# Mixing layer of a hybrid encoder: V's products ahead of the scan's masked ones, masked products of four groups in one run, three scan outputs begun early

## The chip, the cores and the metric

The kernel runs on one core of a Trainium2 chip. The metric is the device time of one execution in microseconds (us); for each kernel the median of several runs is given, and one more execution is profiled. The engines are named as in the profile: PE is the matrix engine, PEld its weight loads, DVE, ACT and POOL the three engines for elementwise work, SP the one that issues transfers (DMAs).

## The reference, cut to what matters

One encoder layer on 512 tokens of width 1024, all in float32. A projection feeds a two-way state-space scan (SSD, 8 groups of 4 heads, chunks of 128 tokens) and a windowed attention (16 heads); both branches are gated, merged and projected, and an MLP follows. What the change touches are these products:

```python
    cb = jnp.einsum('bclgn,bcsgn->bcgls', c, b)
    y_diag = jnp.einsum('bcgls,bcgrls,bcsgrp->bclgrp', cb, decay, xdt)      # the masked products
    ...
    y_off = jnp.einsum('bclgn,bcgrpn,bcgrl->bclgrp', c, prev, jnp.exp(a_cs))
    return (y_diag + y_off).reshape(Bsz, S, G, R, P)
...
    out = jnp.einsum('bngrqk,bnkgd->bnqgrd', p.astype(v.dtype), vb)          # V's products
...
    y = gated_rmsnorm(y.reshape(Bsz, S, D_INNER), z, norm_w)                 # a norm over each group
    return y.astype(z.dtype) @ w_out
...
        mixed = (g_ssd * y_ssd + g_attn * y_attn) @ w_o[l]
```

## The kernel before, in words

**Products.** A float32 weight or activation is split into a high and a low part (`wh`/`wl`, `h`, `yh`/`yl`), and a product is made of three matmuls (`mm3`, L444 to L448), all at L438 in the profile; transposes are at L442. Such a matmul is 128 rows by 128 columns by 512 and reads `128*128 128x512` in the profile. Small products are made in plain float32; the profile shows two records for each. Two kinds of these write only 64 of the 128 columns and read `128*64`: **V's products** (`attn_values`, tiles `pT` and `V`, 20 matmuls or 40 records for a pair of heads) and the scan's **masked products** (in `outs`, tiles `m` and `x`, 8 matmuls or 16 records for a pair of chunks). They are called narrow here, the others wide. A *run* is a stretch of narrow matmuls on PE with no wide one between.

**Stages.** The program is a list of quanta, each one or several products with their weight chunks. First come the projections of attention and gates, and one group of the scan after another, whose small steps are placed between the quanta: `weigh`, `states0`, `states1`, `prep` (which makes a chunk's mask `m`: its last instruction is L1171 on DVE), `outs(0)` and `outs(1)` (each for two chunks: products with the entering state, tiles `C` and `pv`, then the masked ones), `rms` and `finish`. `rms` sums squares on PE (tiles `sh`, `sl`, `ones_r`), and sends the sums through DRAM: four transfers by SP, L1230, L1231, L1233 and L423, with a power on POOL between the second and the third. `finish` makes the rows `yT` (L1243), and `split_y` their parts `yh` and `yl` (L1290, L1291). Then `ssd_out_quanta` multiplies the 16 rows `y` with 8 column blocks of `w_ssd_out`. Rows 14 and 15 belong to the last group and come late, so the first two blocks are multiplied with rows 0 to 13 only (`most`) and completed in `rest`. `folded_quanta("o")` (the product with `w_o`, by a scheme of seven products) and the MLP follow.

**What sets the order.** `Planner` simulates the engines and fixes the order of each engine's queue. For PE, `next_matmul` takes the earliest matmul whose inputs are ready, and prefers one of the kind that PE is at. A narrow matmul is held back until the inputs of all narrow matmuls of its bank are done (`self.awaited`), as long as another matmul is ready.

**Memory.** Tiles live in 83 slots of 128 x 512 words (`Slots`); weights wait in 3 raw buffers (`wr`) and 3 split ones (`wh`, `wl`), so a raw chunk is loaded when POOL has split the one three before it, and split when PE is through with the one three before. PSUM has 3 banks of kind `pp` and 5 of kind `ps`.

Of the kernel before, what the change touches and what calls it, by code (L numbers as in the profile page):

```python
# [11 lines left out]
F32R = mybir.dt.float32r  # L12
AF = mybir.ActivationFunctionType
ALU = mybir.AluOpType
# [98 lines left out]
class Planner:  # L113
# [13 lines left out]
    def __init__(self, instructions, tags):  # L127
        names = {"PE": "PE", "DVE": "DVE", "Activation": "ACT", "Pool": "POOL", "SP": "SP"}
        self.ins = [i for i in instructions if type(i).__name__ != "BassTilePoolBoundary"]
        self.eng = [names[str(i.engine).split(".")[-1]] for i in self.ins]  # L130
        self.tags = tags
        self.depend()
        self.cost = [self.duration(n) for n in range(len(self.ins))]
        self.kind = [self.matmul_kind(n) if e == "PE" else None for n, e in enumerate(self.eng)]
        self.awaited, banks = {}, {}
        for n, k in enumerate(self.kind):
            if k and k[1]:
                banks.setdefault(self.operands(self.ins[n].outs)[0].tensor.name, []).append(n)
        for bank in banks.values():
            needed = set().union(*(self.pre[n] for n in bank)) - set(bank)  # L140
            self.awaited.update((n, needed) for n in bank)

# [234 lines left out]
class Trunk:  # L377
# [187 lines left out]

    def cm(self, w, c, act, done, eng="pppp"):


        nk = w.shape[1] * 8
        chunks = [(w[c // 128, k0 // 8], 8, 128, eng) for k0 in range(0, nk, 8)]  # L570

        def run(parts):
            ps = self.bank("pp")
# [337 lines left out]
    def attn_scores(self, h):  # L911
# [3 lines left out]
        mx, sm, es = (self.tmp(n, [128, 4], 4) for n in ("mx", "sm", "es"))  # L915
        P = []
        for n in range(4):
# [20 lines left out]
        for n in range(4):  # L938
            p, w = P[n]
            nc.vector.tensor_scalar(p[:, :w], p[:, :w], sm[:, n:n + 1], None, op0=ALU.mult)  # L940
        self.P[h] = P

    def attn_flip(self, h):
        self.T[h] = []
        for n, (p, w) in enumerate(self.P.pop(h)):
# [3 lines left out]
            self.slots.put(p)  # L949
            pT = self.slots.get("pT", (128, 384))  # L950
            (self.nc.vector.tensor_copy if n % 2 else self.nc.scalar.copy)(pT[:, :w], pt[:, :w])
            self.T[h].append((pT, w))

    def attn_values(self, k):
# [4 lines left out]
        for n in range(4):  # L959
            nb = T[0][n][1] // 128  # L960
            for b in range(nb):
                blk = max(n - 1, 0) + b
                v = self.V[blk // 2][:, blk % 2, j * 64:(j + 1) * 64]
                for u in range(2):
                    self.mm(po[u * 64:(u + 1) * 64, n * 128:(n + 1) * 128], v, T[u][n][0][:, b * 128:(b + 1) * 128],
                            b == 0, b == nb - 1)
        for pT, _ in T[0] + T[1]:
            self.slots.put(pT)
        hi, lo = self.slots.get("ah", dtype=F32R), self.slots.get("al", dtype=F32R)
# [112 lines left out]
    def ssd_steps(self, g):  # L1082
# [69 lines left out]
        def prep(c):  # L1152
# [21 lines left out]
            return run  # L1174

        def outs(j):

            def run():
                cs = (1, 0) if j == 0 else (2, 3)
                w = st["w"][j]  # L1180
                yos = {}
                for c in cs:
                    yo = yos[c] = self.bank("ps").rearrange("p (d i t) -> p d i t", d=2, i=2)
                    for d in dirs[3 - c]:
                        for i in range(2):
                            S = st["enter"][c][:, d * 256 + i * 128:d * 256 + (i + 1) * 128]
                            self.mm(yo[:, d, i], S, st["C"][:, c * 128:(c + 1) * 128], True, True)
                yd = self.bank("ps").rearrange("p (c i t) -> p c i t", c=2, i=2)
                for c in cs:
                    x, m = xs(c), ch[c]["m"]  # L1190
                    for i in range(2):
                        for u in range(2):
                            h = 2 * i + u
                            self.mm(yd[u * 64:(u + 1) * 64, c % 2, i], x[:, h * 64:(h + 1) * 64], v4(m)[:, h], True, True)
                    put(m)
                for c in cs:
                    dd = slice(dirs[3 - c][0], dirs[3 - c][-1] + 1)
                    E = ch[c]["E"]
                    nc.vector.tensor_tensor(E[:, dd], yos[c][:, dd], E[:, dd], op=ALU.mult)
                nc.vector.tensor_tensor(w, yd, w, op=ALU.add)  # L1200
                for c in cs:
                    wc, E = w[:, c % 2], ch[c]["E"]
                    for d in dirs[3 - c]:
                        nc.gpsimd.tensor_tensor(wc, wc, E[:, d], op=ALU.add)  # L1204
                    nc.gpsimd.tensor_tensor(wc, wc, st["z"][j][:, c % 2], op=ALU.mult)
                    put(E)
                if "ssq" not in st:
                    st["ssq"] = get("ssq")
                sq = get("sq", (128, 2, 2, 128))
                nc.scalar.activation(sq, w, AF.Square)  # L1210
                half = st["ssq"][:, j * 256:(j + 1) * 256].rearrange("p (c t) -> p c t", c=2)
                nc.gpsimd.tensor_tensor(half, sq[:, :, 0], sq[:, :, 1], op=ALU.add)
                put(sq)
                if j == 1:
                    put(st["B"], st["C"], *st["bt"], *st["x"], *st["z"], *st["pv"])
                    hi, lo = st["sq"] = get("sh", dtype=F32R), get("sl", dtype=F32R)
                    self.split(hi, lo, st["ssq"])
                    put(st["ssq"])
            return run
# [33 lines left out]
    def place_head(self, h, q):  # L1253
# [5 lines left out]
        if h % 2:  # L1259
            self.at(at(HEADS["values"]), lambda: self.attn_values(h // 2))  # L1260

# [20 lines left out]
    def split_y(self, k0, k1):  # L1282
        nc = self.nc
        if k0 == 0:
            for hi, lo in self.h:
                self.slots.put(hi, lo)
            self.slots.put(*self.tables)
        for k in range(k0, k1):
# [6 lines left out]
    def ssd_out_done(self, ps, n):  # L1295
# [12 lines left out]
        self.slots.put(t)  # L1308
        self.combine("o", n // 2)
        if n == 7:  # L1310
# [4 lines left out]
    def ssd_out_quanta(self):  # L1315
# [11 lines left out]
        def rest(parts):  # L1327
            wh, wl = parts[0]
            for m, ps in enumerate(banks):
# [3 lines left out]
                self.ssd_out_done(ps, m)  # L1333

        tail = w[0:MIX_ORDER[1] + 1:MIX_ORDER[1], 1, :, 6:8].rearrange("m p k n -> p m (k n)")
        return [Quantum([(w[m, 0], 8, 128, YLO[n]), (w[m, 1, :, :6], 6, 128, YLO[n])], most) for n, m in enumerate(MIX_ORDER[:2])] + [
            Quantum([(tail, 2, 256, "p")], rest)] + [
            self.cm(w, m * 128, lambda: self.ys, lambda ps, n=n: self.ssd_out_done(ps, n), YLO[n]) for n, m in enumerate(MIX_ORDER) if n > 1]

# [334 lines left out]
    def build(self):  # L1674
        self.Q, self.P, self.T, self.bt, self.at_ = {}, {}, {}, {}, []
        self.gate, self.grp, self.yT, self.ys = {}, {}, [], []
        self.h2t, self.h2, self.f, self.acc, self.x1d = [], [], {}, {}, {}
# [27 lines left out]
        c0 = n()  # L1705
        self.at(c0, lambda: self.split_y(0, 14))
        self.add(*self.ssd_out_quanta())
# [43 lines left out]
```

## Time and profile before

| | us |
|---|---|
| median of 3 runs | 1078.82 |
| lowest and highest of them | 1078.32, 1078.97 |
| the profiled execution | 1078.3 |
| its span in the profile | 1076.5 |
| granted clock of PE over the span | 0.998 |

1.8 us of the profiled execution lie outside its span. In the timeline, a row has the start, the time until the last instruction of the row ended, the engine, line, operation, tiles, form and count. Ends of matmuls are modelled and overlap the next one's start, so the time that a matmul takes up on PE is read from start to start.

The scan lasts until about 610 us of the span, the product with `w_ssd_out` from there to 698 us, and `w_o` and the MLP to the end.

### The profile page before, as it was taken

What the parts mean: (1) busy time and instruction counts of PE and PEld (TensorE: products, weight loads), DVE (VectorE), ACT (ScalarE), POOL (GpSimd) and SP (SyncE); (2) the same over time, 40 slices, a digit from 0 to 9 for tenths busy, and PEclk for the clock granted to TensorE, in tenths of its full rate; (3) what the DMA queues carried; (4) which work ended last, traced back from release to release, by engine and by line L of the source; (5) the groups of instructions that cost most, each with busy time, mean ns of one, the idle gap of its engine ahead of it and who ended that gap; (6) DMA issues with size and microseconds to landing.
All of it is one profiled execution on the core that took longest, in us unless ns stands there. A gap on an engine that the chain in (4) does not pass through costs nothing.

```text
span 1076.5 us, 16682 instructions
## 1 busy us (share of the span) xinstructions
PE 1066.9 (99%) x5542; PEld 895.6 (83%) x5542; DVE 761.2 (71%) x1363; ACT 655.5 (61%) x1409; POOL 798.3 (74%) x991
## 2 busy tenths in 40 slices
PE   9999999999999999999999999999999999999997
PEld 7888888888888888888888888889888888888885
DVE  5777787797787788787778543698663574574698
ACT  7756786777686867676769432456555444444552
POOL 5846558467668899988998965215587898898994
PEclk9999999999999999999999999999999999999999
DMA  8334423433434535243554544317321431424222
GB/s 284 117 101 118 119 81 116 130 101 113 122 112 130 152 113 170 95 151 116 156 140 150 167 146 137 108 52 263 98 69 61 155 98 59 157 94 151 70 98 78
DMA packets 61382, 133.21 MB, mean 124 GB/s; under 512 B 9064, under 2 KB 18792, under 8 KB 61296
## 3 DMA queue, kind: packets, MB, share of 16 engines
q1 hardware_dynamic: 61008, 131.76, 39.3%
q8 instruction: 43, 0.70, 0.3%
q10 hardware_dynamic: 288, 0.39, 0.1%
q14 instruction: 43, 0.35, 0.1%
HBM read 127.63 MB, written 4.49 MB: 123 GB/s over the span
## 4 chain that ended last, share of the span: by engine, by line
PE 96%; DVE 1%; DMA 1%; issue 0%; ACT 0%; POOL 0%; SPq 0%; POOLq 0%; DVEq 0%
PE pp L438 66%; PE ps L438 27%; PE ps L442 3%; DMA wr<-in_wv 1%; PE pp L442 0%; DVE P L940 0%; DVE x L1385 0%; DVE acc L1364 0%; SPq L678 0%; DVE wl L608 0%; DVE ag L1664 0%; DVE h L1372 0%; POOLq L1747 0%; ACT wh L605 0%; POOL mrs L1378 0%
## 5 line engine op out<-in xcount | busy, mean ns | idle before, releaser
L517 POOL TENSOR_TENSOR wl<-wr,wh 128x256 fp32r<-128x256 f32 (+1 forms) x517 | 417.3, 837 | 179.8 <-ACT wh L513 176.4
L438 PE MATMUL pp<-h,wh 128*128 128x512 f32 (+1 forms) x1728 | 525.7, 386 | 0.0
L438 PEld LDWEIGHTS pp<-h,wh 128*128 128x128 f32 x1728 | 318.3, 188 | 61.9 <-issue 1.2
L438 PE MATMUL pp<-h,wl 128*128 128x512 f32 (+1 forms) x864 | 333.7, 386 | 0.0
L513 ACT CAST wh<-wr 128x1024 fp32r<-128x1024 f32 x130 | 135.3, 1041 | 120.6 <-PE pp L438 105.9
L438 PEld LDWEIGHTS pp<-h,wl 128*128 128x128 f32 x864 | 162.6, 188 | 31.8 <-issue 0.2
L1590 POOL TENSOR_TENSOR wl<-wd,wh 128x256 fp32r<-128x256 f32 x158 | 130.7, 864 | 11.8 <-ACT wh L1587 11.8
L1587 ACT CAST wh<-wd 128x512 fp32r<-128x512 f32 x92 | 53.2, 618 | 38.4 <-PE pp L438 19.8
L438 PE MATMUL ps<-wl,fh 128*128 128x512 f32 x184 | 71.8, 390 | 0.0
L438 PE MATMUL ps<-wh,fl 128*128 128x512 f32 x184 | 71.7, 390 | 0.0
L438 PE MATMUL ps<-wh,fh 128*128 128x512 f32 x184 | 71.7, 390 | 0.0
L1425 DVE SCALAR_TENSOR_TENSOR pp<-pp,r 128x256 f32<-128x256 f32 (+1 forms) x31 | 17.3, 559 | 66.1 <-ACT r L1422 65.9
L1168 ACT ACTIVATE n<-cb,tables 128x128 f32<-128x128 f32 x128 | 49.3, 391 | 20.6 <-DVE cb L1159 15.2
L1002 DVE SCALAR_TENSOR_TENSOR u<-pp,cv,u 128x510 f32<-128x510 f32 (+1 forms) x64 | 47.7, 746 | 7.0 <-ACT u L998 5.8
L1169 ACT ACTIVATE m<-cb,tables 128x128 f32<-128x128 f32 x128 | 48.9, 388 | 3.8 <-DVE cb L1159 3.6
L438 PE MATMUL pp<-yl,wh 128*128 128x512 f32 x128 | 49.7, 390 | 0.0
L438 PE MATMUL pp<-yh,wl 128*128 128x512 f32 x128 | 49.7, 389 | 0.0
L438 PE MATMUL pp<-yh,wh 128*128 128x512 f32 x128 | 49.5, 390 | 0.0
L1164 ACT ACTIVATE rf<-rf,tables 128x128 f32<-128x128 f32 x128 | 42.5, 392 | 6.6 <-DMA rf<-csT 6.6
L934 ACT ACTIVATE P<-P,mx 128x384 f32<-128x384 f32 (+1 forms) x64 | 35.2, 553 | 15.9 <-DVE mx L931 15.8
L1204 POOL TENSOR_TENSOR w<-w,E 128x256 f32<-128x256 f32 x48 | 38.7, 820 | 7.6 <-DVE w L1200 6.4
L1100 POOL TENSOR_TENSOR xd<-x,tables 128x256 f32<-128x256 f32 x48 | 32.5, 695 | 15.8 <-ACT x L1025 12.8
(279 smaller groups left out, 2160.1 us busy)
## 6 DMA issues: line engine op xcount, KB each, us to landing
wr<-in_w_in_b SPq DMA_DIRECT2D x74, 512.0 KB, 4.0
wr<-in_w_mlp_in_b SPq DMA_DIRECT2D x32, 512.0 KB, 3.5
wd<-in_w_mlp_out SPq DMA_DIRECT2D x64, 256.0 KB, 4.6
rf<-csT SPq DMA_DIRECT2D x32, 256.0 KB, 4.0
rb<-csT SPq DMA_DIRECT2D x32, 256.0 KB, 4.2
wr<-in_w_ssd_out_b SPq DMA_DIRECT2D x14, 512.0 KB, 3.6
x<-in_x SPq DMA_DIRECT2D x16, 256.0 KB, 5.1
E<-csE SPq DMA_DIRECT2D x32, 128.0 KB, 4.6
```

The source lines that it names most:

```text
L438: self.nc.tensor.matmul(out, lhsT, rhs, start=start, stop=stop, skip_group_check=more)
L513: self.nc.scalar.copy(hi[:, :m], raw)
L517: engines[e].tensor_tensor(lo[:, c], raw[:, c], hi[:, c].bitcast(F32), op=ALU.subtract)
L934: nc.scalar.activation(p[:, :w], p[:, :w], AF.Exp, bias=mx[:, n:n + 1], accum_out=sm[:, n:n + 1])
L1002: nc.vector.scalar_tensor_tensor(u[:, a:e], ps[:, a + d:e + d], self.wtap(t, b), u[:, a:e], op0=ALU.mult, op1=ALU.add)
L1100: nc.gpsimd.tensor_tensor(v4(xd[:, d * 256:(d + 1) * 256]), v4(xs(c)), by_dir(self.coef, c)[:, d].unsqueeze(2).to_broadcast([128, 4, 64]), ...
L1164: nc.scalar.activation(v4(rf)[:, h], v4(rf)[:, h], AF.Identity, bias=ncs[:, 0, h:h + 1])
L1168: nc.scalar.activation(v4(n)[:, h], cb[:, 0], AF.Copy, scale=dt[:, 0, h:h + 1])
L1169: nc.scalar.activation(v4(m)[:, h], cb[:, 1], AF.Copy, scale=dt[:, 1, h:h + 1])
L1204: nc.gpsimd.tensor_tensor(wc, wc, E[:, d], op=ALU.add)
L1587: nc.scalar.copy(hi, src)
L1590: (nc.vector if q == 512 else nc.gpsimd).tensor_tensor(lo[:, c], src[:, c], hi[:, c].bitcast(F32), op=ALU.subtract)
```

## The change

V's products are no longer made at a place of their own but are kept in a list, `due`, and made in the next `outs`, ahead of its masked products (the last pair of heads, `ALONE`, excepted). In groups 3, 4, 6 and 7 (`JOINED`) `outs(0)` makes only the products with the entering state, and `outs(1)` the masked products of all four chunks. The planner's rule of waiting now holds for a whole run, in the order in which the program is written, and not for a bank. Each head takes three slots and not four for its probabilities `P`, and three for their transposes `pT`: blocks 0 and 3, both 256 wide, share one. Of the product with `w_ssd_out` three blocks and not two are begun before rows 14 and 15 are there; the other five use `ps` banks; the blocks are taken in another order, and a pair's number in `combine` follows from its block. `split_y` is placed in three parts, 6, 4 and 2 quanta ahead of this product and no more at its start, and the last group's `rms` and `finish` one step later. The number of matmuls, and of instructions on DVE and ACT, stays; POOL has two more (the weight parts of the third block are cut at another place).

```diff
-MIX_ORDER = (0, 4, 1, 5, 2, 6, 3, 7)
+MIX_ORDER, MOST = (0, 4, 2, 6, 1, 5, 3, 7), 3
+SPLIT_Y = ((0, 5, 6), (5, 10, 4), (10, 14, 2))
+Y_BANK = ["ps"] * 8
+PAIRS = (1, 0), (2, 3)
+JOINED = (3, 4, 6, 7)
+ALONE = (7,)
-LAST = dict(SCAN, prep=(0, 1, 3, 4), outs=(2.5, 5.5), rms=8, finish=10)
+LAST = dict(SCAN, prep=(0, 1, 3, 4), outs=(2.5, 5.5), rms=9, finish=11)
...
-        self.awaited, banks = {}, {}
+        self.awaited, n0 = {}, None
+        self.runs, last = [], None
         for n, k in enumerate(self.kind):
-            if k and k[1]:
-                banks.setdefault(self.operands(self.ins[n].outs)[0].tensor.name, []).append(n)
...
+            if k is None:
+                continue
+            if k[1] and last == n0:
+                self.runs[-1].append(n)
+            elif k[1]:
+                self.runs.append([n])
+            n0 = n
+            last = n if k[1] else None
+        for run in self.runs:
+            needed = set().union(*(self.pre[n] for n in run)) - set(run)
+            self.awaited.update((n, needed) for n in run)
...
-            p = self.slots.get("P", (128, 384))
+            own.append(own[0] if n == 3 else self.slots.get("P"))
+            p = own[n][:, 256:] if n == 3 else own[n]
...
+        def diag(j):
+            yd = ch[j]["yd"] = self.bank("ps").rearrange("p (c i t) -> p c i t", c=2, i=2)
+            for c in PAIRS[j]:
+                x, m = xs(c), ch[c]["m"]
+                for i in range(2):
+                    for u in range(2):
+                        h = 2 * i + u
+                        self.mm(yd[u * 64:(u + 1) * 64, c % 2, i], x[:, h * 64:(h + 1) * 64], v4(m)[:, h], True, True)
+                put(m)
...
             def run():
+                off(j)
+                if j == 0 and g in JOINED:
+                    scaled(0)
+                    return
+                while self.due:
+                    self.attn_values(self.due.pop(0))
+                js = (0, 1) if g in JOINED else (j,)
+                for i in js:
+                    diag(i)
+                scaled(j)
+                for i in js:
+                    joined(i)
             return run
...
-            self.at(at(HEADS["values"]), lambda: self.attn_values(h // 2))
+            self.at(at(HEADS["values"]), lambda: self.attn_values(h // 2) if h // 2 in ALONE else self.due.append(h // 2))
...
-        self.combine("o", n // 2)
+        self.combine("o", m % 4)
...
-        return [Quantum([(w[m, 0], 8, 128, YLO[n]), (w[m, 1, :, :6], 6, 128, YLO[n])], most) for n, m in enumerate(MIX_ORDER[:2])] + [
-            Quantum([(tail, 2, 256, "p")], rest)] + [
...
+        return [Quantum([(w[m, 0], 8, 128, YLO[n]), (w[m, 1, :, :6], 6, 128, YLO[n])], most) for n, m in enumerate(first)] + [
+            Quantum([(tail, MOST, 256, "p" * MOST)], rest)] + [
+            self.cm(w, m * 128, lambda: self.ys, lambda ps, n=n: self.ssd_out_done(ps, n), YLO[n], Y_BANK[n])
+            for n, m in enumerate(MIX_ORDER) if n >= MOST]
...
-        self.at(c0, lambda: self.split_y(0, 14))
+        self.at(c0, lambda: self.slots.put(*sum(self.h, ()), *self.tables))
+        for a, b, lead in SPLIT_Y:
+            self.at(c0 - lead, lambda a=a, b=b: self.split_y(a, b))
```

Off, scaled and joined hold the rest of the old `outs` (products with the entering state; the product with `E` on DVE; the sums on DVE, POOL and ACT), unchanged.

How the instructions stand on PE at one place, `outs(0)` of the scan's group 2. Before, its masked products (`m`, `x`) are a run, a wide product of `C` with `B` follows, and then a run of V's products of heads 12 and 13 (the first two rows of 20):

```order
L438 MATMUL ps_3613<-m_3341,x_2864 64x128 x4
L438 MATMUL ps_3613<-m_3480,x_2864 64x128 x4
L438 MATMUL ps_3666<-C_3031,B_2816 128x128
L438 MATMUL ps_3732<-pT_3305,V_69 64x128
L438 MATMUL ps_3732<-pT_3551,V_69 64x128
```

In the change, V's products of heads 10 and 11, which were a run of their own before, stand ahead (the last three rows of 20), and the masked ones follow them with nothing between:

```order
L450 MATMUL ps_3559<-pT_3071,V_70 64x128
L450 MATMUL ps_3559<-pT_2846,V_70 64x128
L450 MATMUL ps_3559<-pT_3071,V_70 64x128
L450 MATMUL ps_3584<-m_3290,x_2818 64x128 x4
L450 MATMUL ps_3584<-m_3428,x_2818 64x128 x4
L450 MATMUL ps_3637<-C_3008,B_2795 128x128
```

One run holds both kinds now; those of heads 12 and 13 stand in the next such run, with `outs(1)`. In group 6, one of the joined ones, PE's queue before has the masked products of two chunks as a run of 16 records among wide ones, and those of the other two chunks some hundred rows later:

```order
L438 MATMUL pp_6271<-al_1055,wh_6069 128x512
L438 MATMUL ps_6194<-C_5852,pv_5992 128x128 x2
L438 MATMUL ps_6197<-m_6007,x_5780 64x128 x4
L438 MATMUL ps_6197<-m_6122,x_5780 64x128 x4
L438 MATMUL ps_6248<-C_5852,B_5757 128x128
```

In the change all four chunks stand together:

```order
L450 MATMUL pp_6454<-h_101,wl_6256 128x512
L450 MATMUL ps_6369<-m_5975,x_5748 64x128 x4
L450 MATMUL ps_6369<-m_6090,x_5748 64x128 x4
L450 MATMUL ps_6378<-m_6201,x_5758 64x128 x4
L450 MATMUL ps_6378<-m_6279,x_5758 64x128 x4
L454 MATMUL ps_6494<-ident,B_6310 128x128 x4
```

Counted over PE's whole queue, before has 23 runs: 7 with V's products of one pair of heads alone, one with a pair and masked products, and 15 with the masked products of one `outs`. The change has 13: two with two pairs and masked products, three with one pair and masked products, one with a pair alone, four with the masked products of four chunks, three with those of two. The first 370 matmuls and the last 1736 of 5097 stand in the same order in both.

SP's queue, where the last group's sums go through DRAM between weight loads (`wr`, of `w_ssd_out`), before:

```order
L1230 DMA rrow_7166<-rstd_7163 1x512
L493 DMA wr_7095<-in_w_ssd_out_b 128x768
L493 DMA wr_7216<-in_w_ssd_out_b 128x2x256
L493 DMA wr_7218<-in_w_ssd_out_b 128x1024
L1231 DMA rcol_7165<-rrow_7166 128x4
L493 DMA wr_7274<-in_w_ssd_out_b 128x1024
L1233 DMA rrow_7166<-rcol_7165 128x4
L493 DMA wr_7276<-in_w_ssd_out_b 128x1024
L423 DMA rstd_7163<-rrow_7166 128x512
```

and in the change:

```order
L1262 DMA rrow_7195<-rstd_7192 1x512
L1576 DMA wd_7579<-in_w_o 128x512
L505 DMA wr_7245<-in_w_ssd_out_b 128x3x256
L1263 DMA rcol_7194<-rrow_7195 128x4
L505 DMA wr_7247<-in_w_ssd_out_b 128x1024
L505 DMA wr_7319<-in_w_ssd_out_b 128x1024
L1265 DMA rrow_7195<-rcol_7194 128x4
L505 DMA wr_7321<-in_w_ssd_out_b 128x1024
L435 DMA rstd_7192<-rrow_7195 128x512
```

Five weight loads stood between the first and the last of the four transfers, four weight loads and one of `w_o` do now. On PE, 110 matmuls stand before from the first of `rms` to the first that reads row 14, and 96 in the change, since `rms` now stands behind the first block.

More of the change, by code (lines that the diff above doesn't have):

```diff
@@ L940, in attn_scores @@
             nc.vector.tensor_scalar(p[:, :w], p[:, :w], sm[:, n:n + 1], None, op0=ALU.mult)
-        self.P[h] = P
+        self.P[h] = P, own[:3]
     def attn_flip(self, h):
-        self.T[h] = []
-        for n, (p, w) in enumerate(self.P.pop(h)):
+        P, own = self.P.pop(h)
+        T = self.T[h] = [], [self.slots.get("pT") for _ in range(3)]
+        for n, (p, w) in enumerate(P):
             pt = self.bank("ps")
@@ new lines, in scaled, with joined @@
+        def scaled(j):
+            for c in PAIRS[j]:
+                dd = slice(dirs[3 - c][0], dirs[3 - c][-1] + 1)
+                E = ch[c]["E"]
+                nc.vector.tensor_tensor(E[:, dd], ch[c]["yo"][:, dd], E[:, dd], op=ALU.mult)
+        def joined(j):
+            w = st["w"][j]
+            nc.vector.tensor_tensor(w, ch[j]["yd"], w, op=ALU.add)
+            for c in PAIRS[j]:
+                wc, E = w[:, c % 2], ch[c]["E"]
+                for d in dirs[3 - c]:
+                    nc.gpsimd.tensor_tensor(wc, wc, E[:, d], op=ALU.add)
+                nc.gpsimd.tensor_tensor(wc, wc, st["z"][j][:, c % 2], op=ALU.mult)
+                put(E)
+            if "ssq" not in st:
+                st["ssq"] = get("ssq")
+            sq = get("sq", (128, 2, 2, 128))
+            nc.scalar.activation(sq, w, AF.Square)
+            half = st["ssq"][:, j * 256:(j + 1) * 256].rearrange("p (c t) -> p c t", c=2)
+            nc.gpsimd.tensor_tensor(half, sq[:, :, 0], sq[:, :, 1], op=ALU.add)
+            put(sq)
+            if j == 1:
+                put(st["B"], st["C"], *st["bt"], *st["x"], *st["z"], *st["pv"])
+                hi, lo = st["sq"] = get("sh", dtype=F32R), get("sl", dtype=F32R)
+                self.split(hi, lo, st["ssq"])
+                put(st["ssq"])
@@ L1188, in run @@
[L1188 to L1199, printed above, removed]
```

74 lines of the change are left out of this document (24 added, 50 removed).

## Prediction

> **What bounds the kernel now.** I read the page's first parts, then the waits of PE, then PE's busy time by stage.
>
> ```profile
> PE 1066.9 (99%) x5542; PEld 895.6 (83%) x5542; DVE 761.2 (71%) x1363; ACT 655.5 (61%) x1409; POOL 798.3 (74%) x991
> PEclk9999999999999999999999999999999999999999
> PE 96%; DVE 1%; DMA 1%; issue 0%; ACT 0%; POOL 0%; SPq 0%; POOLq 0%; DVEq 0%
> ...
> PE pp L438 <- DVE two L663: 1.0, 1, 1.0
> PE ps L442 <- DVE P L940: 0.3, 1, 0.3
> PE ps L438 <- ACT h L463: 0.2, 1, 0.2
> ...
> 300.00:400.00 100.00, 100.00 (x570) 83.98 (x567) 79.03 (x127) 73.48 (x172) 81.19 (x102) 1.00 0.42 124
> 600.00:640.00 40.00, 40.00 (x178) 33.10 (x177) 18.46 (x22) 16.01 (x22) 32.58 (x41) 1.00 0.51 161
> 640.00:700.00 60.00, 60.00 (x266) 49.73 (x265) 31.98 (x62) 24.03 (x39) 26.12 (x36) 1.00 0.41 128
> ```
>
> PE is the bound: 96% of the chain that ended last, 1.5 us of waits in all, no idle time in the stages that change (100.00 of 100.00; 40.00 of 40.00; 60.00 of 60.00), and a granted clock of 1.00 there. So time is won only where PE's own queue gets shorter or one of its rare waits goes, and lost where a new wait appears. The change leaves the number of matmuls as it is. What is left is the time between them, and this differs: a busy PE in this view is not a PE at its pace.
>
> **What a run of narrow matmuls costs.** The timeline has a run of 16, one of 40, and the one place where before already has both in one run of 56:
>
> ```profile
> 785.58 5.44 PE ps L438 x24
> ...
> 595.66 0.39 PE L438 MATMUL pp<-h,wl 128*128 128x512 f32 x1
> 595.97 1.09 PE L438 MATMUL ps<-m,x 128*64 128x128 f32 x16
> 597.00 0.73 PE L438 MATMUL pp<-h,wh 128*128 128x512 f32 x2
> 597.57 0.39 PE L438 MATMUL pp<-h,wl 128*128 128x512 f32 x1
> ...
> 338.38 0.39 PE L438 MATMUL pp<-h,wl 128*128 128x512 f32 x1
> 338.70 2.40 PE L438 MATMUL ps<-pT,V 128*64 128x128 f32 x40
> 341.04 0.74 PE L438 MATMUL pp<-h,wh 128*128 128x512 f32 x2
> 341.62 0.40 PE L438 MATMUL pp<-h,wl 128*128 128x512 f32 x1
> ...
> 158.76 0.39 PE L438 MATMUL pp<-h,wh 128*128 128x512 f32 x1
> 159.08 1.09 PE L438 MATMUL ps<-m,x 128*64 128x128 f32 x16
> 160.00 2.35 PE L438 MATMUL ps<-pT,V 128*64 128x128 f32 x40
> 162.29 1.31 PE L442 MATMUL ps<-ident,P 128*128 128x128 f32 x10
> 163.35 0.48 PE L438 MATMUL pp<-h,wh 128*128 128x512 f32 x1
> ```
>
> A wide matmul takes 5.44/24 = 0.227 us from start to start. From the wide one ahead of the run to the third behind it, 597.57 - 595.66 = 1.91 us pass with 16 narrow ones and 341.62 - 338.38 = 3.24 us with 40. The difference, 1.33 us for 24, gives 0.055 us for a narrow one, and 1.91 - 3 x 0.227 - 16 x 0.055 leaves **0.34 us a run** that no matmul accounts for: PE pays at the run's two ends, whatever its length. The joined run confirms it. Up to the next wide start the two single runs take 597.00 - 595.66 = 1.34 and 341.04 - 338.38 = 2.66 us, less 0.23 for the second wide one ahead 3.77 us; the joined one takes 162.29 - 158.76 = 3.53. That is 0.24 us less, and a further 0.12 shows behind each run, where two wide ones take 597.57 - 597.00 = 0.57 and not 0.45: 0.36 for a run less. So a run costs between 0.24 us (if the part behind it stays) and 0.36 us; I take 0.34, which two runs of different length give.
>
> **The change part by part.**
>
> *Runs.* 23 before, 13 in the change, by PE's two queues. Ten fewer: 10 x 0.34 = **3.4 us** off PE's chain (2.4 to 3.6). Nothing covers or hides it, since PE has no slack in that stage.
>
> *Waits in the scan.* One wait of PE there is visible, behind a run of group 1:
>
> ```profile
> 216.04 0.71 PE L442 MATMUL ps<-ident,P 128*128 128x128 f32 x5
> 217.01 0.52 PE L442 MATMUL ps<-ident,P 128*128 128x128 f32 x3 [0.26 <-DVE P L940]
> ```
>
> Five transposes take 0.97 us from start to start, where ten took 163.35 - 162.29 = 1.06 above: 0.44 us late. Since all of the scan's queue is ordered anew, this spot goes; another like it may come. I take **0.4 us** off, with bounds of 0 and 0.5.
>
> *Later places of V's products, masked products of four chunks at once.* They issue nothing more. The results of V's products come up to one `outs` later; what waits for them are ACT and DVE (split of `ah`, `al`) and then products that stand a group later. The products with the entering state free their banks as before, since `scaled(0)` follows at once. POOL's sums of `outs(0)` move behind `outs(1)`; `rms` is one step later for that, in the last group too. Cost nothing on PE, as long as the sums are done a quantum ahead; the cover is 42 wide matmuls or 9.5 us.
>
> *Shared slots, banks, order of the blocks, `split_y` earlier.* No operation more on DVE and ACT; POOL has four pieces of 192 columns in place of one of 256 and one of 512, about 0.1 us, where it is busy 32.58 of 40 us. They act through waits only, and the stage from 640 has none. I take nothing, and bound it below by nothing and above by the largest wait that this stage could show, that of the next part.
>
> *`rms` behind the first block of three.* Here cover is lost. The last group's sums start at PE, go through four transfers, and end in `yh` and `yl` of rows 14 and 15:
>
> ```profile
> 610.73 0.39 PE L438 MATMUL ps<-sh,ones_r 128*128 128x512 f32 x1
> ...
> 612.54 0.24 SPq L1230 DMA_DIRECT2D rrow<-rstd  x1
> 612.87 5.33 SPq L493 DMA_DIRECT2D wr<-in_w_ssd_out_b  x3
> 618.29 0.38 SPq L1231 DMA_DIRECT2D rcol<-rrow  x1
> ...
> 631.50 0.62 ACT L1290 CAST yh<-yT 128x512 fp32r<-128x512 f32 x1
> ...
> 632.66 2.37 DVE L1291 TENSOR_TENSOR yl<-yT,yh 128x512 fp32r<-128x512 f32 x2
> ...
> 635.71 0.84 PE L438 MATMUL pp<-yh,wh 128*128 128x512 f32 x3
> ...
> SPq L493 <- POOL wl L517: 18.6, 8, 4.2
> ```
>
> Row 14's high part is there 632.12 - 610.73 = 21.4 us after the start, the last part 635.03 - 610.73 = 24.3 us. PE has 110 matmuls to do until it needs the first (25.0 us, as the row at 635.71 shows), in the change 96, or 21.8 us, and ten more of other rows, 24.1 us, until it needs the rest. So a chain of the same length would just fit (0.2 us late at its end). It should be a little shorter: SP stood 5.8 us between its first transfer and its second behind three weight loads, of which one is left, with a load of `w_o`; two now stand ahead of the third. I take nothing here.
>
> *Sum.* 3.4 + 0.4 = 3.8 us off. The profiled execution took 1078.3 us (span 1076.5, and 1.8 around it), so it becomes 1074.5; the median of before is 0.5 above that execution, so the median becomes 1078.8 - 3.8 = **1075.0 us**.
>
> **The rivals.**
>
> *A. PE waits for masks.* A run now starts only when all of its masks are ready, and PE's queue is fixed by a simulation that can be wrong. For it: margins are thin.
>
> ```profile
> 437.33 1.09 PE L438 MATMUL ps<-m,x 128*64 128x128 f32 x16
> ...
> 213.54 0.69 DVE L1171 TENSOR_TENSOR m<-m,rf 128x512 f32<-128x512 f32 x1
> ...
> 436.54 1.15 DVE L1171 TENSOR_TENSOR m<-m,rf 128x512 f32<-128x512 f32 x1
> ```
>
> This mask ends at 437.69, 0.1 us before the second half of the run (437.33 + 8 x 0.055) needs it, and the same operation takes 0.69 or 1.15 us. Against it: in 16 masked products no such wait shows before. If a third of the 12 runs with masks is late by 1.15 - 0.69 = 0.46 us, 1.8 us are lost: 1078.8 - 3.4 + 1.8 = 1077.2.
>
> *B. Rows 14 and 15 come late.* One wait of SP for POOL's split of a weight chunk is up to 4.2 us long (last row of the fence above), and three of the four transfers stand behind such a load. If one more such wait falls into the chain, PE stands 4.2 us: 1075.0 + 4.2 = 1079.2, no change. With two, 1083.4, **slower**; it decides from a stall of 3.8 + 2.2 = 6.0 us on. Against it: loads wait there already, and the chain includes 5.8 us of them.
>
> On such a stall the Trainium skill, "TensorE: Matmul & The Clock Gate", section "What's actually happening", says more: an idle window of about 3.4 us halves PE's clock. By that rule a stall of 4.2 us could cost some 1.7 us more (an estimate from the page: one window at half speed). No row here shows PE idle that long in mid-kernel; the clock is 1.00 in all three stages quoted.
>
> *C. The price is not the run's.* If PE paid for a new bank or a new mask and not for a change between wide and narrow, the change would win nothing: 1078.8. Against it stands the run of 56 above, which has two banks and three tiles and pays once.
>
> **How the numbers follow.** Forecast 0.74, A 0.13, B with one wait 0.06, B with two 0.05, C 0.02. The forecast's own range is 1074.2 (ten runs at 0.36, the wait at 0.5, and 0.5 for short waits that the view drops) to 1076.4 (ten runs at 0.24 and no wait gone). Scatter of runs adds 0.3 below, and A lies above: 1073.9 to 1077.3 leaves out B and C, part of A and little below. A measurement of this kernel tells 0.2%, 2.2 us, from no change: faster means below 1076.7, slower above 1081.0. Faster: 0.74 and 0.08 of A, 0.82. Within: the rest of A, one wait of B and C, 0.13. Slower: 0.05.
>
> **What would show it.** PE's records, 5542, and the 0.055 us of a narrow one stay; 13 runs in the timeline, each with 0.24 to 0.36 us at its ends; the scan's last run and `rms`'s neighbour 3 to 4 us earlier; the stage behind 640 us moved, not shortened. The step on rows 14 and 15 is wrong if PE has a wait for `yh` or `yl` some 21 to 25 us after the row of `sh` and `ones_r`; A is right if runs with `m` start late behind L1171 on DVE. The forecast falls if runs at their ends cost much less when they are longer, or if waits of PE add up to over 3 us more than now.

## The result, and the profile after

| | us |
|---|---|
| the change, median of 13 runs | 1076.32 (1074.07 to 1078.17) |
| before, median of 13 runs of the same set | 1078.95 (1078.14 to 1082.13) |
| ratio | 0.9969, 95% interval 0.9958 to 0.998 |
| profiled execution of the change, its span | 1077.91, 1076.1 |

The change is 2.6 us faster by these medians; 1075.0 was predicted, in a range that holds the result. The 1.3 us between them do not lie in the part of the kernel that was changed. Both kernels' executions fall on two levels here. Of the change's, seven lie at 1074.1 to 1076.3 and six at 1077.2 to 1078.2; of before's, nine at 1078.1 to 1079.1 and four at 1081.6 to 1082.1. The median of the change lies at the edge between its two groups. Level against level, by the groups' medians, it is 3.8 us faster on the lower (1074.9 against 1078.7) and 4.0 on the upper (1077.8 against 1081.8).

The profiled execution was one of the upper level. Its engine row and chain, in the page of the change:

```profile
PE 1064.1 (99%) x5542; PEld 895.0 (83%) x5542; DVE 769.1 (71%) x1363; ACT 657.7 (61%) x1409; POOL 797.6 (74%) x993
...
PE 91%; DVE 4%; ACT 2%; issue 1%; DMA 1%; POOL 0%; SPq 0%; DVEq 0%; POOLq 0%; ACTq 0%
```

PE is busy 2.8 us less than before (1066.9), but its share of the chain is 91% and not 96%. What is new, beyond one of 0.2 us, are three waits, in the view of PE's waits (total, times, longest):

```profile
PE pp L450 <- ACT KH L888: 1.2, 1, 1.2
PE ps L450 <- DVE pT L964: 1.1, 1, 1.1
...
PE ps L450 <- DVE Q L914: 0.3, 1, 0.3
```

The timeline of the change leads them back to one instruction, a product in the arithmetic of dt at the start of the program:

```profile
29.93 8.42 POOL L529 TENSOR_TENSOR wl<-wr,wh 128x256 fp32r<-128x256 f32 x12
30.02 1.75 DVE L826 RECIPROCAL dtw<-dtw 128x256 f32<-128x256 f32 x1 [1.64 <-ACT dtw L825]
31.81 7.17 DVE L827 TENSOR_TENSOR dtw<-dtw,dtw 128x256 f32<-128x256 f32 x1
42.97 0.73 PE L450 MATMUL pp<-h,wh 128*128 128x512 f32 x2 [1.19 <-ACT KH L888]
81.11 0.45 PE L450 MATMUL ps<-KH,Q 128*128 128x384 f32 x1 [1.13 <-DVE pT L964]
```

The same instruction in the timeline of before:

```profile
29.70 9.34 POOL L517 TENSOR_TENSOR wl<-wr,wh 128x256 fp32r<-128x256 f32 x12
31.58 0.54 DVE L815 TENSOR_TENSOR dtw<-dtw,dtw 128x256 f32<-128x256 f32 x1
```

In the chain of the change that ended last, the product is followed at once by the parts of K, `KL` and `KH`; PE's wait at 42.97 is for a later `KH` of the same series:

```profile
38.98 0.61 DVE KL L887
39.61 0.58 ACT KH L888
```

The product took 0.54 us before and 7.17 us here, and ended (38.98) 0.6 us behind POOL's series of twelve (38.35), about its own time. POOL needed 0.70 us for each of its instructions where DVE stood still (8.42/12), and 0.78 where both moved (9.34/12). DVE's queue is 6.6 us late behind it. The instruction stands in a stretch whose order the change leaves as it was, so the change did not bring it about in any way that the order shows. The runs below ask where the 4 us come from, and what the level is.

### The profile page after: what moved, and what is told of

Its sections match the earlier page's. It is cut to its first block, busy times and chain, and to the rows that moved or that the text cites. A ratio compares the mean times of both kernels' runs of the same rounds, so it can differ in the third digit from the quotient of the medians.

```text
span 1076.1 us, 16654 instructions
## 1 busy us (share of the span) xinstructions
PE 1064.1 (99%) x5542; PEld 895.0 (83%) x5542; DVE 769.1 (71%) x1363; ACT 657.7 (61%) x1409; POOL 797.6 (74%) x993
## 4 chain that ended last, share of the span: by engine, by line
PE 91%; DVE 4%; ACT 2%; issue 1%; DMA 1%; POOL 0%; SPq 0%; DVEq 0%; POOLq 0%; ACTq 0%
PE pp L450 57%; PE ps L450 31%; PE ps L454 3%; DVE dtw L827 1%; DMA wr<-in_wv 1%; DVE u L1015 0%; ACT P L947 0%; DVE P L938 0%; DVE dtw L831 0%; PE pp L454 0%; DVE KL L887 0%; DVE P L953 0%; ACT h L745 0%; DVE x L1417 0%; DVE Q L914 0%
## 5 line engine op out<-in xcount | busy, mean ns | idle before, releaser
L525 ACT CAST wh<-wr 128x1024 fp32r<-128x1024 f32 (+1 forms) x130 | 135.4, 1041 | 126.5 <-PE pp L450 98.1
L1175 POOL TENSOR_TENSOR rb<-rb,tables 128x512 f32<-128x512 f32 x32 | 36.5, 1142 | 10.0 <-DVE al L468 5.9
L1674 DVE TENSOR_TENSOR acc<-acc,ps 128x512 f32<-128x512 f32 x46 | 31.3, 681 | 15.7 <-PE ps L450 15.5
L1183 DVE TENSOR_TENSOR m<-m,n 128x512 f32<-128x512 f32 x32 | 29.6, 925 | 16.0 <-ACT m L1182 15.5
```

Source lines behind the costliest of these rows:

```text
L525: self.nc.scalar.copy(hi[:, :m], raw)
L1175: nc.gpsimd.tensor_tensor(v4(rb), v4(rb), cs[:, 1].unsqueeze(2).to_broadcast([128, 4, 128]), op=ALU.subtract)
```

## The experiments

Each experiment is written as a short diff. "(13)" and the like count the runs of narrow matmuls. Before was run beside each set: 1078.68 (1077.59 to 1079.92, 21 runs) beside the first four kernels, 1078.49 (1077.87 to 1081.39, 32 runs) beside the next four, 1078.68 (1077.73 to 1081.9, 24 runs) beside the last four.

| kernel | median us (lowest to highest, runs) | ratio to before, 95% interval |
|---|---|---|
| after_again (13) | 1074.72 (1074.33 to 1075.41, 5) | 0.9964, 0.9951 to 0.9976 |
| before_psum (23) | 1078.23 (1077.49 to 1078.84, 11) | 0.9995, 0.9986 to 1.0004 |
| after_psum (13) | 1074.34 (1073.81 to 1074.73, 5) | 0.9959, 0.9947 to 0.9972 |
| runs_23 (23) | 1078.95 (1077.76 to 1079.52, 11) | 1.0002, 0.9993 to 1.0011 |
| dt_late (13) | 1079.68 (1078.96 to 1082.15, 11) | 1.0007, 0.9998 to 1.0016 |
| v_alone (19) | 1077.57 (1076.76 to 1081.51, 11) | 0.9994, 0.9985 to 1.0003 |
| not_joined (17) | 1076.06 (1075.21 to 1076.36, 10) | 0.9975, 0.9966 to 0.9984 |
| two_blocks (13) | 1080.10 (1078.02 to 1080.86, 11) | 1.0008, 0.9999 to 1.0016 |
| three_pp (13) | 1083.12 (1082.43 to 1085.23, 7) | 1.0039, 1.0024 to 1.0054 |
| two_blocks_9 (13) | 1083.36 (1082.72 to 1084.65, 6) | 1.0036, 1.0022 to 1.0051 |
| j_34567 (12) | 1077.74 (1077.31 to 1079.58, 12) | 0.9987, 0.9978 to 0.9997 |
| after_third (13) | 1074.78 (1074.35 to 1079.22, 12) | 0.9970, 0.9957 to 0.9983 |

### The change again, and the dt product out of POOL's way

`after_again` is the change itself. `before_psum` and `after_psum` have two operands of the dt arithmetic in a PSUM bank:

```diff
-        w = [self.dtv] + [get("dtw", (128, 4, 64)) for _ in range(5)]
-        v, e, r, s2, p, al = w
+        w = [self.dtv] + [get("dtw", (128, 4, 64)) for _ in range(3)]
+        v, r, p, al = w
+        half = self.bank("ps").rearrange("p (i c h) -> p i c h", i=2, c=4)
+        e, s2 = half[:, 0], half[:, 1]
```

> The changed kernel once more, to count levels. Theory T (one DVE operation near 32 us of the span, the product dtw<-dtw,dtw, sometimes waits for POOL's whole series of weight splits, in either kernel, and the change is worth 3.9 us at either level): times fall on two levels, about 1074.6 and 1077.8, and before falls on about 1078.6 and 1081.8; nothing in between by more than 0.8. Rival R (the change makes the upper level itself, by V's later products or the shared slots): before stays near 1078.6 in nearly all runs, the change on two levels. Rival S (the levels belong to the chip or the session): all runs of one call fall on one level.

> Before, with the two operands e and s2 of the dt arithmetic in a PSUM bank, so that its DVE products read one operand from SBUF and not two. T: the long product is gone (under 0.8 us in the profile), all runs near 1078.5, none above 1079.6; ratio to before 0.997 to 1.000 by how many of before's runs are on the upper level. R: no word on before's upper level; if before has one at all, this keeps it. S: levels stay, up to 1082.

> The change, with the same edit. T: all runs near 1074.6, none above 1075.6; 3.9 us (3.4 to 4.4) under the edited before. R: still two levels, 1074.6 and 1077.8, as the cause is elsewhere. S: the same two levels.

These four kernels ran on one chip, and no execution there lay on an upper level, before's 21 included; so the two levels that theory T expected did not show. The change took 1074.72 us, 3.96 less than before, and its product of dt took 0.54 us. The edit in PSUM alone is within the noise for both kernels (0.4 us less each), so it changes nothing else and serves as the base of the runs that follow; whether it cures the upper level was not seen, since there was none to cure. But the profile of `after_psum` shows what it does to the two engines:

```profile
29.36 8.41 POOL L529 TENSOR_TENSOR wl<-wr,wh 128x256 fp32r<-128x256 f32 x12
31.15 0.43 DVE L829 TENSOR_TENSOR ps<-ps,dtw 128x256 f32<-128x256 f32 x1
```

With one operand in PSUM the product takes 0.43 us, less than 0.54, and POOL's series beside it 0.70 us for each (8.41/12), as when DVE stood still: here neither delays the other.

### The number of runs

`runs_23` takes all joining out of `after_psum`, `v_alone` that of V's products with masked ones, `not_joined` that of four chunks:

```diff
-JOINED = (3, 4, 6, 7)
-ALONE = (7,)
+JOINED = ()
+ALONE = (0, 1, 2, 3, 4, 5, 6, 7)
```

This is the diff of `runs_23`; `v_alone` has the lines of `ALONE` only, `not_joined` those of `JOINED`.

> The change with the same edit, but all of V's products at their own place and no group joined: 23 runs of narrow matmuls again and not 13, while shared slots, three early blocks, block order and placing of split_y stay. If the price is the run's (0.34 us each): 3.4 us above the edited change, 1078.0, within 0.6 of the edited before. Rival: the gain comes from slots, banks or the early blocks: then it stays near 1074.6.

> after_psum with no group's masked products begun beside V's: each group that shares a run in the change has its own again, 19 runs of narrow products in place of 13, all else kept. Theory of the prediction (each run costs 0.34 us): 1074.3 + 6 x 0.34 = 1076.4 (1075.8 to 1076.5 by 0.24 to 0.36 each). Rival (what 23 runs cost was waits that only that order had): under 1075.0.

> after_psum with no run joined over groups: 17 runs in place of 13, all else kept. Theory of the prediction: 1074.3 + 4 x 0.34 = 1075.7 (1075.3 to 1075.8). Rival (runs cost nothing when all they read is there): 1074.4, no difference that 5 rounds tell.

With 23 runs the change's time is that of before, to 0.3 us (and 0.95 us above the 1078.0 expected), though slots, banks, three blocks, their order and `split_y` are all the change's. So the gain hangs on the joining. The price of a run is read best between two points that lie on either side of the runs, since single profiles differ by 1 us at the program's start: from the first transposes of `P` in PE's timeline to the first product of the norm. In `after_psum`:

```profile
75.86 1.26 PE L454 MATMUL ps<-ident,P 128*128 128x128 f32 x10
...
616.11 0.39 PE L450 MATMUL ps<-sh,ones_r 128*128 128x512 f32 x1
```

In `not_joined`:

```profile
76.97 1.26 PE L454 MATMUL ps<-ident,P 128*128 128x128 f32 x10
...
618.50 0.39 PE L450 MATMUL ps<-sh,ones_r 128*128 128x512 f32 x1
```

In `v_alone`:

```profile
76.69 1.26 PE L454 MATMUL ps<-ident,P 128*128 128x128 f32 x10
...
140.68 0.94 PE L454 MATMUL ps<-ident,P 128*128 128x128 f32 x5 [0.85 <-DVE P L955]
...
620.73 0.39 PE L450 MATMUL ps<-sh,ones_r 128*128 128x512 f32 x1
```

In `runs_23`:

```profile
76.42 1.26 PE L454 MATMUL ps<-ident,P 128*128 128x128 f32 x10
...
621.08 0.39 PE L450 MATMUL ps<-sh,ones_r 128*128 128x512 f32 x1
```

`after_psum` takes 540.25 us for this stretch, `not_joined` 541.53: 1.28 us for four more runs, **0.32 us each**. `v_alone` takes 3.79 us more for six. At 0.32 the runs make 1.9 of it; 0.85 is the wait in the row at 140.68, on the softmax's DVE for transposes right behind a run, 0.2 is one more wait that the profile shows, and 0.8 is not traced. `runs_23` takes 4.41 us more for ten: 3.2 for the runs, 0.3 for a wait, and 0.9 not traced. If the untraced part were the runs' too, one would cost 0.41 to 0.45 us in these two kernels, where V's products have runs of their own; so the price is sure to about 0.1 us. The medians say the same less sharply, since these kernels ran on two chips: not_joined 1076.06 - 1074.34 = 1.7, runs_23 4.6. So the expectation for `not_joined` was right on the stretch (its median lies 0.3 us above the range), the one for `v_alone` 1.2 us too low, and 0.85 of that is a wait that it had not foreseen. Neither before nor `runs_23` has a wait at that place, so those 0.85 us belong to the order of `v_alone` and are no part of the gain.

### The late product by hand

```diff
-        nc.vector.reciprocal(r, r)
+        for _ in range(5):
+            nc.vector.reciprocal(r, r)
```

> after_psum with its reciprocal of dt written four times more (4 x 1.75 us = 7.0 us more of DVE ahead of the next product of dt, nothing else changed; the value is the same). It sets by hand the lateness that the first profile of the change had (that product took 7.17 us in place of 0.54). Theory T (that lateness alone is the 3 us between the two levels of times): 1076.8 to 1078.0, and PE waits of some 2.5 us at 43 to 81 us. Rival (the product's lateness is covered, and the levels have another cause): 1074.0 to 1074.9, as after_psum with 1074.34.

The median is 5.3 us above `after_psum`: the rival is out, lateness there is not covered, and it costs more than theory T gave. Its profiled execution was the slowest of its eleven, 2.5 us above their median. PE's waits in it:

```profile
PE ps L450 <- DVE Q L917: 2.8, 1, 2.8
PE pp L450 <- DVE yl L1322: 2.6, 1, 2.6
PE ps L450 <- DVE pT L967: 1.1, 1, 1.1
```

The first and the third (2.8 + 1.1) follow from the late product; the remaining 1.4 of the 5.3 us are not traced. (The ten other executions have a mean clock of 0.996 to 0.997, the profiled one 0.998; a clock that is halved for some 3 us would give that, but none of the ten was profiled.) The second is of another kind; the timeline of `dt_late`:

```profile
616.62 6.64 DVE L1322 TENSOR_TENSOR yl<-yT,yh 128x512 fp32r<-128x512 f32 x1 [6.04 <-ACT yh L1321]
617.14 5.58 POOL L529 TENSOR_TENSOR wl<-wr,wh 128x192 fp32r<-128x192 f32 x9
```

The part `yl`, 1.1 us in the change's second profile, took 6.64 us beside a series of nine instructions of POOL, and ended (623.26) 0.5 us behind it (622.72). So the fault of the first profile has come again at another product, with the size by which that execution lay above the rest (2.6 against 2.5 us).

### The levels, once more

> The change itself, a third time, for the two levels of times. Theory T (an upper level is one execution in which a DVE product of two tiles waits out a series of POOL, like the 7.17 us in the first profile and 6.64 us in that of dt_late): lower level 1074.1 to 1075.4, upper one 1077.2 to 1078.2, mixed within one chip, and independent of what before shows; a profile on the upper level has such a DVE row, one on the lower level has none that PE waits for. Theory S (the level belongs to the chip): all executions of one chip on one level.

Seven executions lay at 1074.35 to 1074.79, five at 1078.06 to 1079.22, mixed on one chip, so theory S is out. How often the upper level comes may still differ by chip: of the 26 executions of the change and of before in the first set none lay there. Rival R is out too, since before has upper executions without the change: four of 13 in the result's set, and eleven of 56 above 1080.4 us beside the last eight kernels. Theory T had the place of the upper level too low: 1077.2 to 1078.2 was expected, and three of the five lie above. The profiled one was of the upper level, and its timeline has the same row as the first:

```profile
29.81 8.40 POOL L529 TENSOR_TENSOR wl<-wr,wh 128x256 fp32r<-128x256 f32 x12
31.69 7.15 DVE L827 TENSOR_TENSOR dtw<-dtw,dtw 128x256 f32<-128x256 f32 x1
```

Of three profiles of the change two are on the upper level and have it; the third, `after_again`, is on the lower and does not. By the spans of the first profile and of `after_again`, 1076.1 and 1073.0, the upper level is 3.1 us longer, and the three waits make 2.6 of it. What decides in an execution whether DVE gets its turn is not shown. Whether the edit in PSUM keeps a kernel off the upper level was not tested side by side; what there is speaks for it at this product, since on the chip where five of twelve executions of the change lay there, none of the twelve of `j_34567` (below), which has the edit, lies more than 1.9 us above its median. It does not cure other products, as `yl` in `dt_late` shows. Nor was an execution of before on its upper level profiled; that it has the same cause is likely, since the instructions there are the same, but only argued.

### Blocks and banks

`two_blocks` puts back before's blocks, banks, `split_y` and `rms` in `after_psum`; `two_blocks_9` is the same with the change's `rms`; `three_pp` changes only the banks:

```diff
-MIX_ORDER, MOST = (0, 4, 2, 6, 1, 5, 3, 7), 3
-SPLIT_Y = ((0, 5, 6), (5, 10, 4), (10, 14, 2))
-Y_BANK = ["ps"] * 8
-LAST = dict(SCAN, prep=(0, 1, 3, 4), outs=(2.5, 5.5), rms=9, finish=11)
+MIX_ORDER, MOST = (0, 4, 1, 5, 2, 6, 3, 7), 2
+SPLIT_Y = ((0, 14, 0),)
+Y_BANK = ["pp"] * 8
+LAST = dict(SCAN, prep=(0, 1, 3, 4), outs=(2.5, 5.5), rms=8, finish=10)
```

This is the diff of `two_blocks`; `two_blocks_9` is without the lines of `LAST`, and `three_pp` has those of `Y_BANK` only.

> after_psum with two blocks of scan outputs begun before the end of the scan in place of three, in the numbering of before, and with y's split as before: 13 runs as in the change. Theory of the prediction (the third block and the numbering are worth nothing by themselves): 1074.0 to 1074.8. Rival (the third block covers the norm behind the scan): 0.5 to 3.0 us more, 1074.9 to 1077.3, with a wait of PE for the norm's scale at about 670 us.

> after_psum with the other five blocks of the product with w_ssd_out in pp banks again, as before the change; three blocks are still begun ahead of rows 14 and 15, but no fourth can be, since there are three pp banks. From the first product of sh and ones_r PE then has 86 matmuls, 19.5 us, until it needs row 14, whose high part took 21.2 us to come in the second profile of the change (616.96 to about 638.2). Theory C (the chain of the norm is only just covered, and the ps banks are what covers it): a wait of PE of 1.5 to 2 us there, and one of up to 2.2 us behind it for a pp bank, as two_blocks had: 1075.8 to 1078.3. Rival (the prediction's: banks are worth nothing by themselves): 1074.0 to 1074.9.

> two_blocks with the last group's rms and finish at the change's place, one step later. Theory C: the 0.8 us wait for sh goes, and what is left is the missing cover, as in three_pp: 1075.8 to 1078.3, and within 0.7 us of three_pp, since the third block alone gives PE no matmul more. Rival (two_blocks lost its time to sums that were asked for a step too early): 1074.0 to 1075.0.

The first expectation failed on both sides: `two_blocks` is 5.8 us above `after_psum` by the median, and the wait is not at 670 us. PE's waits in the profile of `two_blocks`:

```profile
PE pp L450 <- DVE ft L1489: 2.2, 1, 2.2
...
PE ps L450 <- ACT sh L467: 0.8, 1, 0.8
```

The second is the sums of the last group, asked for a step before they are done, since `JOINED` puts them off; the first is a bank that is still to be emptied at 642 us. The two make 3.0 of the 4.7 us by which the span (1076.8) exceeds that of `after_psum` (1072.1). Theory C was right on the place and too low on the size, by 5 us: the two kernels with the change's `rms` and without its banks take 1083, **4.4 us more than before**, and differ by 0.24 us. The waits of PE in `three_pp`:

```profile
PE pp L450 <- DVE ft L1489: 4.0, 1, 4.0
PE pp L450 <- ACT yh L1320: 1.6, 1, 1.6
```

The 1.6 us for row 14 are what was expected. The wait for a bank behind it is 4.0 and not 2.2 us, since the first bank is done later by the first wait. The rest is told by the timeline of PE and by the windows of PE (length; busy time with count of PE, PEld, DVE, ACT and POOL; granted clock; DMA share; GB/s):

```profile
641.91 0.39 PE L450 MATMUL pp<-yh,wl 128*128 128x512 f32 x1
646.33 0.69 PE L450 MATMUL pp<-yh,wh 128*128 128x512 f32 x1 [4.04 <-DVE ft L1489]
646.82 0.63 PE L450 MATMUL pp<-yl,wh 128*128 128x512 f32 x1
647.24 0.63 PE L450 MATMUL pp<-yh,wl 128*128 128x512 f32 x1
...
650.08 0.40 PE L450 MATMUL pp<-yh,wh 128*128 128x512 f32 x1
650.31 0.39 PE L450 MATMUL pp<-yl,wh 128*128 128x512 f32 x1
```

```profile
640.00:646.00 6.00, 2.30 (x11) 1.56 (x9) 4.82 (x11) 1.99 (x5) 3.34 (x6) 1.00 0.30 89
...
647.00:648.00 1.00, 1.00 (x4) 0.80 (x3) 0.93 (x3) 0.26 (x1) 0.00 (x0) 0.50 0.40 70
648.00:649.00 1.00, 1.00 (x4) 0.71 (x4) 1.00 (x4) 0.37 (x1) 0.00 (x0) 0.50 0.91 360
```

Behind the wait of 4.0 us PE's clock is 0.50, and a matmul takes 0.43 us and not 0.227, until 650.08: nine take 650.08 - 646.33 = 3.75 us instead of 2.04, 1.7 us more. (In `two_blocks` the wait was 2.2 us and the clock stayed at 1.00 in the profile, of 1078.78 us; of its eleven executions the four at 1078.0 to 1078.8 have a mean clock of 0.998 to 0.999, the seven at 1079.9 to 1080.9 one of 0.996 to 0.997. A clock halved for some 3 to 4 us would give both, but none of the seven was profiled.) So 1.6 + 4.0 + 1.7 = 7.3 of the 8.4 us by which the span of `three_pp` (1080.5) exceeds that of `after_psum` (1072.1).

### One more run joined

```diff
-JOINED = (3, 4, 6, 7)
+JOINED = (3, 4, 5, 6, 7)
```

> after_psum with group 5's masked products in one run too: 12 runs in place of 13. By the price of a run, 0.34 to 0.43 us (not_joined lost 1.7 us with four more): 1073.9 to 1074.0. Rival (a new wait takes it back, as in v_alone, where 1.2 and 0.7 us of waits came with six more runs): 1074.6 or more.

One run fewer lost 3.4 us by the median, so the rival was right. PE's waits in its profile:

```profile
PE pp L450 <- POOL wl L529: 0.7, 1, 0.7
PE ps L450 <- DVE xl L1120: 0.5, 1, 0.5
PE ps L450 <- ACT sh L467: 0.4, 1, 0.4
```

All of them stand between 560 and 566 us of its timeline, where four chunks' sums of group 5 come to POOL at once and its split of weights stands behind them. They make 1.6 us; from the first transposes of `P` (76.33) to the first product of the norm (619.50) the kernel takes 2.9 us more than `after_psum`, and the rest is not traced to single waits. So joining is free, as far as these runs show, where POOL has room for the sums that it puts off; the prediction's proviso for this part ("as long as the sums are done a quantum ahead") is broken there, and holds in the four groups that the change joins.

No kernel here is shown to be faster than the change: `after_psum` lies 0.4 us below it, within both intervals.

## Why the prediction was right, step by step

*Runs, 3.4 us.* Right in mechanism and size. A run of 32 records, a length that before does not have, in the timeline of `after_again`:

```profile
431.97 0.39 PE L450 MATMUL pp<-h,wl 128*128 128x512 f32 x1
432.19 0.61 PE L450 MATMUL pp<-h,wh 128*128 128x512 f32 x2
432.74 1.97 PE L450 MATMUL ps<-m,x 128*64 128x128 f32 x32
434.64 0.50 PE L450 MATMUL pp<-h,wl 128*128 128x512 f32 x1
434.97 0.62 PE L450 MATMUL pp<-h,wh 128*128 128x512 f32 x2
435.44 0.40 PE L450 MATMUL pp<-h,wl 128*128 128x512 f32 x1
```

3.47 us from the first row to the last, less six wide ones (1.36) and 32 narrow ones at 0.055 (1.76), leave 0.35 us: the price of a run of 16 or 40. By `not_joined` it is 0.32.

*Waits in the scan, 0.4 us.* Right that the wait for `P` goes: the profile of `after_again` has no wait of PE in the scan. How the gain divides between runs and waits is sure only to about 1 us, since 0.9 us of what `runs_23` loses is not traced.

*The sum.* Before's last matmul starts at 1068.29 us, that of `after_again` at 1064.99; their first transposes of `P` at 76.20 and 76.70. So the stretch that was changed is 3.8 us shorter: 3.8 was the sum. The medians of the change's lower level in its three sets (1074.9, 1074.72 and 1074.44) are 0.1 to 0.6 us below the forecast.

*What missed by 1.3 us* is the step from the sum to the median: the sum was made against a profile in which the dt product took 0.54 us, and no term stood for the executions in which it takes 7. The prediction knew a level only from three runs of before within 0.65 us. With five of twelve or six of thirteen executions 3 to 4 us higher, a median falls anywhere between 1074.7 and 1078.

*`rms` behind the first block: nothing.* Right, and the closest call of all. The timeline of `after_again`:

```profile
616.96 0.39 PE L450 MATMUL ps<-sh,ones_r 128*128 128x512 f32 x1
...
637.56 1.13 ACT L1318 CAST yh<-yT 128x512 fp32r<-128x512 f32 x2
638.21 1.96 DVE L1319 TENSOR_TENSOR yl<-yT,yh 128x512 fp32r<-128x512 f32 x2 [0.84 <-ACT yh L1318]
638.77 0.84 PE L450 MATMUL pp<-yh,wh 128*128 128x512 f32 x3
...
641.03 0.39 PE L450 MATMUL pp<-yl,wh 128*128 128x512 f32 x1
```

PE comes to row 14 after 638.77 - 616.96 = 21.8 us and to the low parts after 24.1, both as worked out. The high part is there after 21.2 us, the low parts after 23.2: 0.6 and 0.9 us to spare.

*Banks, blocks, slots: nothing.* Right for the change as it stands, wrong as a statement on the parts. That the stage had no wait said only that its cover was enough, not that it was ample. The 96 matmuls of cover include ten of a fourth block, which can begin only because it has a `ps` bank; without that bank (`three_pp`) 86 were left, and 8.8 us were lost. The bound given, "the largest wait that this stage could show, that of the next part", was meant for rival B; `three_pp` shows where B ends, with a late row 14, a late bank and a slow clock, but not B's cause: the chain is no longer than in the change (row 14's high part comes 21.2 us after its start in both), and it is the cover that is shorter. That its 1083.1 us lie near the 1083.4 worked out for two waits of SP is chance.

*The clock.* The prediction set beside B the Trainium skill's rule ("TensorE: Matmul & The Clock Gate", section "What's actually happening"): an idle window of about 3.4 us halves PE's clock, some 1.7 us more as an estimate. No row of before could show it; `three_pp` does, with 0.50 for some 3 us and 1.7 us lost behind 4.0 us of waiting. The wait of 2.8 us in the profile of `dt_late` left the clock at 1.00. So trace and rule agree as far as the profiles go.

*Rival A* did not occur: no wait of PE in `after_again` is for a mask. *Rival C* fell with `runs_23` and `not_joined`.

*What would show it.* The records are 5542 as said, the joined runs cost what they should, and PE has no wait for `yh` or `yl`. The last run of the scan starts 3.0 us earlier (592.95 in place of 595.97), 3.5 when the starts of the two profiles are set equal. From there to the last matmul 472.3 us pass before and 472.0 in `after_again`: the end is moved, not shortened, as said.

## What to carry to other kernels

Here a stretch of matmuls of another width cost PE about a third of a microsecond at its ends, whatever its length (16, 32 or 40 records), so gather such matmuls, and count the stretches to price it; but ask of each thing put off for it which engine then has it all at once. Where a stage has no waits, ask how much cover it has left before calling an edit there free: a bank that wins nothing by itself can be what makes another edit possible. And before a forecast is set against a median, look whether executions fall on levels; a median between two levels moves with their mix.

## What the runs showed of the hardware that was not expected

An elementwise product of DVE with two operands in SBUF took 6.6 us longer than the 0.54 us of other executions beside a series of POOL's products that ran back to back, and ended half a microsecond behind its end (7.17 and 7.15 us; at another place, where 1.1 us is usual, 6.64). The Trainium skill ("SBUF — State Buffer", sections "SBUF: two separate sides" and "Who interferes with whom") states that such a DVE instruction contends with a GpSimd one that reads SBUF, through an exclusive lock held for the whole instruction. The rows agree that one waits for the other, but not for how long: one POOL instruction is 0.70 us, and DVE waited for about nine of them. In the profiles of the lower level both engines move and each is a little slower (0.54 us for DVE, 0.78 for POOL) than with one of DVE's operands in PSUM (0.43 and 0.70 in `after_psum`).
